# Eight resident GLA states instead of seven, with the stacked keys of both stream parities in one tile

## The chip, the core and the metric

The kernel runs on one core of a Trainium2 chip, in one launch. The metric is device time in microseconds. The core has a matrix engine (PE in the profile, with its weight loads as PEld), a vector engine (DVE), a scalar engine (ACT), a general engine (POOL), a queue engine (SP), and DMA engines that these feed. Each engine works through its own instructions in the order in which the program lists them and waits, by semaphores, for what the others produce. Three runs of the kernel before took 2575.13, 2565.62 and 2572.58 us; their median, 2572.58 us, is the time to compare with.

## What is computed

A step of a two-layer encoder. Layer 0 is stick-breaking attention, layer 1 gated linear attention (GLA). There is one new stream of 512 tokens (the prompt) and eight running streams of 16 new tokens each (the samples), all at width 2048. The change touches layer 1's samples. For each of 4 heads a stream has a state matrix of 256 x 512, which is read for the output, decayed, and extended by the new tokens' keys and values:

```python
def gla_chunk(S, inp):
    q, k, v, g = inp
    C = q.shape[1]
    b = jnp.cumsum(g, axis=1)
    b_last = b[:, -1]
    q_in = q * jnp.exp(b)
    a = jnp.einsum('bchd,bshd->bhcs', q_in, k * jnp.exp(-b))
    a = jnp.where(jnp.tril(jnp.ones((C, C), dtype=bool)), a, 0.0)
    o = jnp.einsum('bhcs,bshe->bche', a, v) + jnp.einsum('bchd,bhde->bche', q_in, S)
    S = jnp.exp(b_last)[..., None] * S + jnp.einsum('bshd,bshe->bhde', k * jnp.exp(b_last[:, None] - b), v)
    return S, o
```

The samples' states come in as `state_gla` and leave as the output `s_sample`, in float32. Each is cut into two pieces of 128 x 512 (256 KB), so 64 pieces pass through the core: 8 streams, 4 heads, 2 pieces. Two layer projections, normalisations and the output projection surround this.

## The kernel before

**The whole.** All products are made of float32 numbers split into a high and a low part (`halves`, L133 to L135), three matmuls for a product. The kernel has a main stream of matmuls (projections), and lanes of side work (attention, GLA) that it slips between them. In layer 1's GLA stage the main stream is first `plain` (L620 to L652; its matmuls are L641), which makes the remaining queries and keys with 320 columns a matmul, then `share` (L673 to L724; matmuls L687, 512 columns), which is the output projection head by head. The main stream's matmul output is `ps_mm`; the lanes use `ps_tp` and `ps_z`.

**Who sets the order.** PE's order is written by the kernel itself. `pe["now"]` is a running estimate of PE's time, and `Side.tick` (L316 to L333) lets a lane take its next step when the estimate has reached the time that the lane asked for with `step`. `Side.after` puts off a call by a given time. So what a lane asks for decides where in the main stream its matmuls stand. The orders of DVE, ACT, POOL and SP are made by a scheduler when the program is built. [...]

**The sample lane** (`sample_lane`, L1761 to L1846). For each head it makes queries (`qz`) and stacked keys, then goes through four groups n = 0 to 3. A group is one 128-row piece `dt` of the state (n // 2) and one parity `e` of the streams (n % 2), that is four states, of streams e, 2 + e, 4 + e and 6 + e. In a group:

- Four matmuls at L1825 read the four states for the output. Each has 32 columns of weights, and the four stand in four column strips of PE's array. In the profile they are 8 instructions, since a float32 matmul is two.
- Four matmuls at L1831 make the four updates, each of 512 columns. Their weights are `kst[e][:, m, :]` and the moving operand is `vst[:, m, :]`. `kst` is two tiles: in `kst0` only rows 0 to 47 hold keys, in `kst1` only rows 64 to 111; the other rows are zero. `vst` holds the values of even streams in rows 0 to 47 and of odd ones in rows 64 to 111. All 128 rows take part, and the zeros drop the other parity.
- DVE adds the update to the decayed state (L1833), and `leaves` (L1756) stores the state and, 7.0 units of the estimate later, asks for the next load.

**The states' places.** A state piece lies in a tile `s0` (called `s` in the profile) of a ring of `S0 = 7` tiles. Seven loads are asked for at the start (L1753), each later one by `leaves`. A load into a place must wait until the store of the state that was there has landed. Loads and stores of states, the gate tiles (`gate`, in and out), `vst` and the prompt's state `S` all go by `move` (L76 to L78), which is a DMA issued by POOL, so they stand in one line, in order, with POOL's small arithmetic (`on_r`, L234). A group waits in the estimate until all its four states have been asked for 8.0 units ago.

**The key tile.** `stack` (L1790 to L1807) transposes the keys into a bank and copies rows 0 to 47 with ACT and rows 64 to 111 with DVE into `kst[0]` and `kst[1]`.

**From `plain` to `share`.** When `plain` ends, `share` for head 0 needs four tiles of rows (`og_in`, loaded by SP, L1857), each split into `ogh` (ACT) and `ogl` (DVE). The prediction calls the stretch between the two the seam.

```python
                    for m in range(4):
                        yield step(0.3, tp=1)
                        pt = bank("tp")
                        l = kst[e][:, m, :]
                        mm(pt, l, by(l, vst[:, m, :]), start=True, stop=True)
```

## Time and profile before

| | |
|---|---|
| median of three runs | 2572.58 us |
| the profiled execution | 2576.88 us, of which the span from the first to the last instruction is 2575.1 us |
| PE busy | 2454.8 us (95%), 17369 matmuls |
| DVE, ACT, POOL busy | 1592.8, 1016.3, 163.4 us |
| GLA stage | from about 2050 us to 2452 us of the span |
| L1825 and L1831 in it | 128 and 64 instructions on PE |
| state loads and stores | 64 and 64, of 256 KB each, 4.5 and 4.0 us median from issue to landing |

A row of the timeline gives the start, the duration, the engine, the line, the operation, what is written and read, the shape and a count; in brackets how long the engine had been idle and what ended that. On PE a shape such as `128*32` is the rows and columns of weights. A matmul's end is modelled and overlaps the next one, so the time that a matmul takes from the engine is the distance between the starts of two rows, not the duration. In the rows on waits the columns are the engine, what it was about to write and its line, then what it waited for; total us, times, longest. In the rows by window: the window, its length, busy time (and instructions) of PE, PEld, DVE, ACT and POOL, the clock granted to PE as a share of full speed, the share of time that the DMA engines were busy, and GB/s.

### The profile page before, as it was taken

How to read it: one execution, taken by the hardware profiler on the slowest of the kernel's cores; microseconds unless marked ns; L12 is line 12 of the kernel's file. 1: busy time of each engine (PE TensorE's matmuls, PEld its weight loads, DVE VectorE, ACT ScalarE, POOL GpSimd, SP SyncE). 2: the span in 40 equal slices, each digit the busy share in tenths (PEclk: the TensorE clock that was granted, in tenths of full speed). 3: DMA queues.
4: the chain of work that ended last, by engine and by line, in shares of the span. 5: the costliest groups of instructions: out<-in, count | busy, mean ns of one | idle time of the engine just before them, and what ended most of it. 6: DMA issues, size and time to landing. Idle time of an engine off the chain costs nothing.

```text
span 2575.1 us, 43490 instructions
## 1 busy us (share of the span) xinstructions
PE 2454.8 (95%) x17369; PEld 2160.0 (84%) x17369; DVE 1592.8 (62%) x2469; ACT 1016.3 (39%) x1794; POOL 163.4 (6%) x385
## 2 busy tenths in 40 slices
PE   6899999999999999999999889999999999979998
PEld 4579999998999988777777767999999988857776
DVE  5565555555666656766776577665667565555456
ACT  4332222222223335565444344333333554555223
POOL 0010000000000000000000000000000233242000
PEclk7899999999999999999999999999999999989999
DMA  9956666766654366766665763345443777785633
GB/s 341 324 190 218 223 210 200 237 213 195 218 190 122 115 209 210 231 214 205 221 222 173 228 214 121 99 115 141 121 117 110 213 224 245 233 280 191 208 118 144
DMA packets 452797, 502.06 MB, mean 195 GB/s; under 512 B 26090, under 2 KB 349810, under 8 KB 452466
## 3 DMA queue, kind: packets, MB, share of 16 engines
q1 hardware_dynamic: 429634, 435.55, 53.5%
q0 software_dynamic: 16048, 51.92, 6.1%
q10 hardware_dynamic: 6912, 11.80, 1.2%
q8 instruction: 137, 2.24, 0.4%
q14 instruction: 66, 0.54, 0.1%
HBM read 410.05 MB, written 89.13 MB: 194 GB/s over the span
## 4 chain that ended last, share of the span: by engine, by line
PE 77%; DMA 9%; DVE 7%; issue 3%; ACT 3%; POOL 1%; SPq 0%; ACTq 0%; DVEq 0%; POOLq 0%
PE ps_mm L583 39%; PE ps_mm L687 10%; PE ps_mm L641 6%; PE ps_mm L367 3%; PE ps_mm L507 3%; DMA ar<-in_w_ada_dram 2%; PE ps_tp L1061 2%; PE ps_z L180 1%; PE ps_tp L1516 1%; PE ps_tp L1029 1%; PE ps_z L1005 1%; DVE wl L135 1%; DMA gv<-kr 1%; PE ps_tp L1106 1%; PE ps_mm L1965 1%
## 5 line engine op out<-in xcount | busy, mean ns | idle before, releaser
L583 PE MATMUL ps_mm<-sums,wh 128*128 128x320 f32 x2752 | 618.0, 313 | 5.8 <-ACT wh L134 5.8
L583 PEld LDWEIGHTS ps_mm<-sums,wh 128*128 128x128 f32 x2752 | 462.1, 189 | 14.9 <-ACT wh L134 7.1
L583 PE MATMUL ps_mm<-h,wh 128*128 128x320 f32 x2064 | 462.7, 312 | 3.0 <-DVE u L589 2.8
L583 PE MATMUL ps_mm<-sums,wl 128*128 128x320 f32 x1376 | 428.0, 311 | 1.0 <-DVE wl L135 1.0
L135 DVE TENSOR_TENSOR wl<-wr,wh 128x1024 fp32r<-128x1024 f32 x194 | 237.2, 1223 | 239.2 <-ACT wh L134 238.2
L583 PEld LDWEIGHTS ps_mm<-h,wh 128*128 128x128 f32 x2064 | 344.0, 188 | 19.0 <-issue 13.7
L134 ACT CAST wh<-wb 128x1024 fp32r<-128x1024 f32 x170 | 178.4, 1050 | 426.9 <-PE ps_mm L583 370.4
L134 ACT CAST wh<-wr 128x1024 fp32r<-128x1024 f32 x194 | 203.6, 1050 | 339.3 <-PE ps_mm L583 179.1
L583 PE MATMUL ps_mm<-h,wl 128*128 128x320 f32 x1032 | 319.4, 310 | 0.2 <-DVE wl L135 0.2
L641 PE MATMUL ps_mm<-h,wh 128*128 128x320 f32 x1152 | 268.7, 320 | 8.9 <-ACT wh L134 5.4
L583 PEld LDWEIGHTS ps_mm<-sums,wl 128*128 128x128 f32 x1376 | 260.5, 189 | 1.8 <-DVE wl L135 1.8
L135 DVE TENSOR_TENSOR wl<-wb,wh 128x1024 fp32r<-128x1024 f32 x170 | 207.7, 1222 | 60.9 <-ACT wh L134 60.5
L641 PEld LDWEIGHTS ps_mm<-h,wh 128*128 128x128 f32 x1152 | 195.7, 192 | 26.0 <-issue 12.1
L687 PE MATMUL ps_mm<-wh,ogh 128*128 128x512 f32 x460 | 200.0, 435 | 5.7 <-DVE y L692 2.8
L583 PEld LDWEIGHTS ps_mm<-h,wl 128*128 128x128 f32 x1032 | 194.2, 188 | 0.5 <-DVE wl L135 0.5
L687 PE MATMUL ps_mm<-wh,ogl 128*128 128x512 f32 x460 | 181.9, 395 | 0.5 <-DVE ogl L135 0.5
L687 PE MATMUL ps_mm<-wl,ogh 128*128 128x512 f32 x460 | 181.8, 395 | 0.0
L641 PE MATMUL ps_mm<-h,wl 128*128 128x320 f32 x576 | 180.1, 313 | 1.4 <-DVE wl L135 1.4
L687 PEld LDWEIGHTS ps_mm<-wh,ogh 128*128 128x128 f32 x460 | 87.6, 190 | 33.5 <-issue 16.5
L641 PEld LDWEIGHTS ps_mm<-h,wl 128*128 128x128 f32 x576 | 110.2, 191 | 2.1 <-DVE wl L135 2.1
L943 DVE TENSOR_TENSOR_SCAN k<-k,zero_c 128x544 f32<-128x544 f32 (+4 forms) x96 | 93.2, 975 | 29.4 <-ACT k L939 16.6
L687 PEld LDWEIGHTS ps_mm<-wh,ogl 128*128 128x128 f32 x460 | 87.1, 189 | 20.8 <-DVE ogl L135 0.9
(352 smaller groups left out, 3773.9 us busy)
## 6 DMA issues: line engine op xcount, KB each, us to landing
ar<-in_w_ada_dram SPq DMA_DIRECT2D x160, 512.0 KB
wb<-in_sb_w_in_dram SPq DMA_DIRECT2D x82, 512.0 KB
kc<-in_cache_sb_k_dram SPq DMA_DIRECT2D x64, 512.0 KB
vc<-in_cache_sb_v_dram SPq DMA_DIRECT2D x64, 512.0 KB
wr<-in_gla_w_in_dram SPq DMA_DIRECT2D x51, 512.0 KB
wb<-in_gla_w_in_dram SPq DMA_DIRECT2D x45, 512.0 KB
wr<-in_sb_w_in_dram SPq DMA_DIRECT2D x44, 512.0 KB
ar<-in_w_ada_dram SPq DMA_DIRECT2D x64, 256.0 KB
```

The lines of the kernel that those rows point to most:

```text
L134: nc.scalar.copy(hi, x)
L135: (e or dve).tensor_tensor(lo, x, hi.bitcast(F32), op=ALU.subtract)
L180: mm(acc[32 * q:32 * q + 32, :w], cT[:, kt + m, :], by(cT[:, kt + m, :], rs[m // each][:, m % each, q, :]), start=kt + m == 0, stop=kt + m ...
L367: mm(acc[a], l[:, c], by(l[:, c], r[:, k2, :]), start=kt == k0 and first, stop=kt == k0 + nk - 1 and last)
L507: mm(acc[a], l, by(l, r[:, e, :]), start=j == 0 and e == 0 and begun, stop=j == 7 and e == 1 and last)
L583: mm(acc, l[:, k, :], by(l[:, k, :], r), start=start and k == 0 and first, stop=k == 7 and last, skip_group_check=True)
L641: mm(acc[nt], l[:, k, :], by(l[:, k, :], r), start=k0 == 8 and k == 0 and first, stop=k0 == 0 and k == 7 and last)
L687: mm(acc, l, by(l, r[:, e, :]), start=i == 0 and e == 0 and first, stop=i == 1 and e == 1 and last)
L943: dve.tensor_tensor_scan(kr, kr, zeros[:, :w], 1.0, ALU.mult, ALU.add)
L1005: mm(z[:, :n], q[:, hh, qs], by(q[:, hh, qs], k[:, hh, :n]), start=True, stop=True)
L1029: mm(o[:, :P], l, by(l, aT[:, kb, :]), start=kb == 0, stop=kb == qb)
L1061: turn_block(tp[:, P * c:P * c + P], block(kc[:, c, P * hh:P * hh + P]), ident)
```

## The change

`S0` becomes 8. The place for the eighth state (512 float32 a partition) comes from `kst`, which is now one tile instead of two of that size: even streams' keys stay in its rows 0 to 47, odd ones' in 64 to 111, and each update's matmul takes only the 64 rows of its parity, of `kst` and of `vst`. One zeroing of a tile by POOL at the stage's start goes.

```diff
-S0 = 7
+S0 = 8
...
-        kst = [gl.tile([P, 4, P], F32R, name=f"kst{n}") for n in range(2)]
+        kst = gl.tile([P, 4, P], F32R, name="kst")
         vst = gl.tile([P, 4, 512], F32R, name="vst")
-        for t in qz + kst + [vst]:
+        for t in qz + [kst, vst]:
             nc.gpsimd.memset(t.bitcast(F32), 0.0)
...
-                        (dve.tensor_copy if e else nc.scalar.copy)(kst[e][r], tp[r].rearrange("p (m n) -> p m n", m=4))
+                        (dve.tensor_copy if e else nc.scalar.copy)(kst[r], tp[r].rearrange("p (m n) -> p m n", m=4))
...
-                        l = kst[e][:, m, :]
-                        mm(pt, l, by(l, vst[:, m, :]), start=True, stop=True)
+                        l = kst[64 * e:64 * e + 64, m, :]
+                        mm(pt, l, by(l, vst[64 * e:64 * e + 64, m, :]), start=True, stop=True)
```

The number of places is part of what the lane's requests depend on, so PE's order in the GLA stage moves too, and the orders of the other engines with it.

PE, head 0, from the last update of the first group on. The names are matmul output, moving operand and weights; a number tells one tile of a name from another, `s_...` being a state's place. Before:

```order
L1831 MATMUL ps_tp<-vst,kst_20571 128x512
L641 MATMUL ps_mm<-h,wh 128x320 x2
L641 MATMUL ps_mm<-h,wl 128x320
...
L1528 MATMUL ps_tp<-q,k 128x128 x2
L1676 MATMUL ps_tp<-ident,k 128x128 x2
...
L1825 MATMUL ps_z<-s_20593,qz_20570 32x512
L1825 MATMUL ps_z<-s_20595,qz_20570 32x512
L1825 MATMUL ps_z<-s_20597,qz_20570 32x512
L1825 MATMUL ps_z<-s_21319,qz_20570 32x512
```

And now:

```order
L1831 MATMUL ps_tp<-vst,kst 128x512
L1825 MATMUL ps_z<-s_20591,qz_20570 32x512
L1825 MATMUL ps_z<-s_20593,qz_20570 32x512
L1825 MATMUL ps_z<-s_20595,qz_20570 32x512
L1825 MATMUL ps_z<-s_20597,qz_20570 32x512
L641 MATMUL ps_mm<-h,wh 128x320 x2
L641 MATMUL ps_mm<-h,wl 128x320
...
L1563 MATMUL ps_tp<-ident,on 128x128 x4
L1831 MATMUL ps_tp<-vst,kst 128x512
```

The second group used to stand 24 main matmuls after the first one's last update, since its fourth state (`s_21319`) had to take a place that the first group left; it now follows at once. In every head groups 0 and 1 form a pair, and groups 2 and 3 form another, 84 main matmuls after the first one (45 of the longer ones in the last head).

PE at the seam, head 2, from the end of `plain` to the first matmuls of `share`. Before:

```order
L641 MATMUL ps_mm<-h,wl 128x320
L1831 MATMUL ps_tp<-vst,kst_20571 128x512 x4
L1563 MATMUL ps_tp<-ident,on 128x128 x4
L1600 MATMUL ps_tp<-alr_in,wa_22793 128x320 x2
L687 MATMUL ps_mm<-wh,ogh 128x512
L687 MATMUL ps_mm<-wl,ogh 128x512
L687 MATMUL ps_mm<-wh,ogl 128x512
L1825 MATMUL ps_z<-s_23397,qz_20570 32x512
L1825 MATMUL ps_z<-s_23399,qz_20570 32x512
L1825 MATMUL ps_z<-s_23401,qz_20570 32x512
L1825 MATMUL ps_z<-s_23496,qz_20570 32x512
```

And now:

```order
L641 MATMUL ps_mm<-h,wl 128x320
L1831 MATMUL ps_tp<-vst,kst 128x512
L1825 MATMUL ps_z<-s_23298,qz_20570 32x512
L1825 MATMUL ps_z<-s_23300,qz_20570 32x512
L1825 MATMUL ps_z<-s_23362,qz_20570 32x512
L1825 MATMUL ps_z<-s_23364,qz_20570 32x512
...
L1831 MATMUL ps_tp<-vst,kst 128x512 x2
L1600 MATMUL ps_tp<-alr_in,wa_22825 128x320 x2
L687 MATMUL ps_mm<-wh,ogh 128x512
L687 MATMUL ps_mm<-wl,ogh 128x512
L687 MATMUL ps_mm<-wh,ogl 128x512
```

Head 2's last group and its four updates stood inside `share`'s first products and now stand ahead of them.

POOL, the DMAs for that same group. A name ahead of the arrow is written, `out_7_dram` is the samples' state output, `out_6_dram` the prompt's; the group's states are 23397, 23399, 23401 and 23496 before, and 23298, 23300, 23362 and 23364 now. Before:

```order
L78 DMA s0_23401<-in_state_gla_dram 128x512
L234 TENSOR_TENSOR on_r_23365<-on_ms_23363,mhalf_79 128x1
L78 DMA og_2_93<-gate_23160 512x1x128
L78 DMA out_6_dram<-S_22871 128x2x512
L78 DMA out_7_dram<-s0_23222 128x512
L78 DMA gate_23425<-gr_3_106 128x4x128
L78 DMA out_7_dram<-s0_23287 128x512
L78 DMA out_7_dram<-s0_23289 128x512
L78 DMA out_7_dram<-s0_23373 128x512
L78 DMA og_2_93<-gate_23309 512x1x128
L78 DMA s0_23496<-in_state_gla_dram 128x512
```

And now:

```order
L78 DMA out_7_dram<-s0_22621 128x512
L78 DMA out_7_dram<-s0_22665 128x512
L78 DMA gate_23214<-gr_2_105 128x4x128
L78 DMA s0_23298<-in_state_gla_dram 128x512
L78 DMA s0_23300<-in_state_gla_dram 128x512
L78 DMA s0_23362<-in_state_gla_dram 128x512
L78 DMA s0_23364<-in_state_gla_dram 128x512
L234 TENSOR_TENSOR on_r_23290<-on_ms_23288,mhalf_79 128x1
```

The group's fourth load used to stand behind the four stores of the group just before it and two DMAs of `og`; now all four loads stand behind the stores of the pair before, and ahead of those of their own pair.

## The prediction

> **What bounds the kernel now.** I read the page first, then the stage that the change touches by windows, then the waits, then the timelines of PE, DVE and POOL around each wait. The page:
>
> ```profile
> PE 2454.8 (95%) x17369; PEld 2160.0 (84%) x17369; DVE 1592.8 (62%) x2469; ACT 1016.3 (39%) x1794; POOL 163.4 (6%) x385
> ```
>
> PE is the bound of the whole. The GLA stage by windows:
>
> ```profile
> 2050.00:2207.00 157.00, 153.75 (x982) 137.63 (x980) 94.37 (x170) 81.70 (x160) 51.11 (x86) 1.00 0.74 237
> 2207.00:2220.00 13.00, 8.58 (x37) 6.34 (x35) 6.03 (x14) 5.01 (x10) 4.45 (x9) 0.74 0.72 228
> 2220.00:2283.00 63.00, 63.00 (x400) 56.05 (x399) 36.62 (x67) 31.59 (x63) 20.99 (x36) 1.00 0.74 236
> 2283.00:2310.00 27.00, 11.83 (x34) 5.60 (x34) 16.95 (x28) 14.55 (x26) 10.35 (x17) 0.68 0.83 289
> 2310.00:2452.00 142.00, 138.13 (x638) 108.25 (x637) 76.39 (x121) 60.58 (x103) 30.94 (x53) 1.00 0.60 196
> ```
>
> Outside two holes, at 2207 and 2283, PE is full, and after both holes its clock is low for a while (0.74 and 0.68 as means). So time is won by closing holes, and any time that PE's own instructions gain in the full stretches is paid whole. Who makes the holes:
>
> ```profile
> POOL out_dram L78 <- DVE s L1833: 53.7, 20, 13.4
> POOL s L78 <- DMA out_dram<-s: 25.9, 18, 3.4
> PE ps_z L1825 <- DMA s<-in_state_gla_dram: 17.0, 2, 12.6
> ```
>
> PE waits 17.0 us in two pieces for a state's load, and POOL, which issues it, sits in its line for stores that wait for DVE, and for stores to land ahead of loads.
>
> **What the change takes away: the first hole.** PE there, and an undisturbed group of L1825 for comparison:
>
> ```profile
> 2073.82 0.40 PE L1516 MATMUL ps_z<-v,aNl 128*128 128x512 f32 x1
> 2074.15 1.07 PE L1825 MATMUL ps_z<-s,qz 128*32 128x512 f32 x8
> 2075.14 0.56 PE L641 MATMUL ps_mm<-h,wh 128*128 128x320 f32 x2
> 2075.54 0.31 PE L641 MATMUL ps_mm<-h,wl 128*128 128x320 f32 x1
> 2075.69 0.45 PE L641 MATMUL ps_mm<-h,wh 128*128 128x320 f32 x2
> 2075.98 0.31 PE L641 MATMUL ps_mm<-h,wl 128*128 128x320 f32 x1
> ```
>
> ```profile
> 2206.29 1.06 PE L1825 MATMUL ps_z<-s,qz 128*32 128x512 f32 x6
> 2211.77 1.92 PE L1825 MATMUL ps_z<-s,qz 128*32 128x512 f32 x2 [4.42 <-DMA s<-in_state_gla_dram]
> 2213.61 0.90 PE L641 MATMUL ps_mm<-h,wh 128*128 128x320 f32 x2
> 2216.60 0.31 PE L641 MATMUL ps_mm<-h,wl 128*128 128x320 f32 x1
> ```
>
> A group takes 2075.14 - 2074.15 = 0.99 us; this one took 2213.61 - 2206.29 = 7.32, so 6.33 are lost. Then PE runs at half speed until 2216.60: the same instructions, at the distances of undisturbed ones, would take about 1.7 instead of 2.99 us, which is 1.3 more. The hole costs 7.6 us. Its cause, with the group before on PE:
>
> ```profile
> 2194.19 1.07 PE L1825 MATMUL ps_z<-s,qz 128*32 128x512 f32 x8
> 2196.59 0.75 DVE L1833 SCALAR_TENSOR_TENSOR s<-s,es,ps_tp 128x512 f32<-128x512 f32 x1 [2.49 <-PE ps_tp L1831]
> 2203.44 1.12 POOL L78 DMA_DIRECT2D out_dram<-s  x2
> 2207.04 0.55 POOL L78 DMA_DIRECT2D s<-in_state_gla_dram  x1
> ```
>
> The state whose place is wanted was updated at 2197.3, stored from 2203.4, and reloaded from 2207.0 to 2211.8: 14.4 us from update to the next state, of which 6.1 were POOL's line, while the two groups' reads start 12.1 us apart. In the new order a place is wanted again two groups later. From the start of one pair to that of the next in the same head stand 170 instructions on PE, counted in the order; at the pace of the third window (63.00 us for 400) that is 27 us. In the last head it is 131, at the pace of the fifth window (142.00 for 638) 29 us. 27 against 14.4 leaves 12, so I take the wait as gone, and the low clock behind it with it. Three more groups lose a little, because their four matmuls did not start together:
>
> ```profile
> 2105.53 1.66 PE L1825 MATMUL ps_z<-s,qz 128*32 128x512 f32 x8
> 2119.61 1.45 PE L1825 MATMUL ps_z<-s,qz 128*32 128x512 f32 x8
> 2262.92 1.90 PE L1825 MATMUL ps_z<-s,qz 128*32 128x512 f32 x8
> ```
>
> Against 1.07 that is 0.59 + 0.38 + 0.83 = 1.8 us, which goes for the same reason.
>
> **The second hole, at the seam.** The wait there is the longer one, but something else is late just behind it:
>
> ```profile
> 2289.35 1.93 PE L1825 MATMUL ps_z<-s,qz 128*32 128x512 f32 x6
> 2303.87 1.92 PE L1825 MATMUL ps_z<-s,qz 128*32 128x512 f32 x2 [12.59 <-DMA s<-in_state_gla_dram]
> 2305.71 0.79 PE L687 MATMUL ps_mm<-wh,ogh 128*128 128x512 f32 x1
> 2309.97 0.39 PE L687 MATMUL ps_mm<-wh,ogh 128*128 128x512 f32 x1
> ```
>
> ```profile
> 2291.66 0.81 DVE L135 TENSOR_TENSOR ogl<-og_in,ogh 128x640 fp32r<-128x640 f32 x1
> 2298.29 0.82 DVE L135 TENSOR_TENSOR ogl<-og_in,ogh 128x640 fp32r<-128x640 f32 x1 [0.85 <-ACT ogh L134]
> 2302.84 0.83 DVE L135 TENSOR_TENSOR ogl<-og_in,ogh 128x640 fp32r<-128x640 f32 x1 [0.80 <-ACT ogh L134]
> ```
>
> `share`'s first accumulation needs the second, third and fourth `og` rows, ready at 2292.5, 2299.1 and 2303.7. Without the state's wait PE would do the second at 2292.5, the third at 2299.1, and the fourth from 2303.7, at the low clock (0.43 us a matmul), to 2305.0; with an update of 0.2 the next accumulation would begin at about 2305.2 instead of 2309.97. So of 12.6 us of wait only 4.8 are won; the rest of the hole stays, now as a wait for `og` rows. Bounds: nothing, if the rows come 5 us later than now; 15.4 (2305.71 less 2290.34, the undisturbed end of the group), if they come that much earlier. I take 4.8, since nothing in the rows' own chain (`og_in` loads by SP, then a split each) is edited.
>
> Together the change takes away 7.6 + 1.8 + 4.8 = 14.2 us.
>
> **What it adds: 64 updates in a half-height tile.** The moving operand keeps 512 columns, so L1831 itself is no shorter. What is new is that its weights fill 64 rows, between matmuls of 128. Two kinds of rows bound that. A matmul of 96 rows stands among others of 128 and costs only its columns (320 columns, 0.15 us to the next start, as for L641):
>
> ```profile
> 2313.67 0.31 PE L1600 MATMUL ps_tp<-alr_in,wa 96*128 96x320 f32 x1
> 2313.82 0.40 PE L687 MATMUL ps_mm<-wh,ogh 128*128 128x512 f32 x1
> ```
>
> And tiles of 32 columns cost something on the way in and out. In: 2074.15 - 2073.82 = 0.33 instead of the usual 0.23 for 512 columns, 0.10. Out: 0.40 to the second L641 row instead of 0.29, 0.11. Between: a run of twice the length shows the clean rate,
>
> ```profile
> 56.28 1.93 PE L180 MATMUL ps_z<-ar,cT 128*32 128x256 f32 x32
> 184.62 1.07 PE L222 MATMUL ps_z<-ar,cT 128*32 128x256 f32 x16
> ```
>
> 16 instructions of 256 columns, the work of L1825's 8 of 512, take 1.93 - 1.07 = 0.86, but the group took 0.99: 0.13. One visit to another tile shape costs 0.34 us. The weights now loaded on entry are 128 columns instead of 32:
>
> ```profile
> L1831 PEld LDWEIGHTS ps_tp<-vst,kst x64: 186/188/330, 2077.3 to 2391.4; 128*128 128x128 f32 x64
> L1825 PEld LDWEIGHTS ps_z<-s,qz x128: 106/109/155, 2074.1 to 2388.5; 128*32 128x32 f32 x128
> ```
>
> That may show 0.08 more, 0.42 in all. So a visit costs between 0 (the 96-row matmul) and 0.42; I take 0.38, the middle of 0.34 and 0.42, because a half-height tile is a tile of another shape like L1825's, and the 96-row one is likely still the full array. The Trainium skill speaks to this: TensorEngine Tiling (Array Packing), "Key Properties", says that a change of the tiling mode, not merely of the tile, drains the engine, and its list of modes has 64 x 128 apart from 128 x 128 and none of 96. By that rule the visit is paid, as in L1825's rows; the 96-row row does not contradict it; no row of this case shows a 64-row tile.
>
> How many visits: in the new order the 64 updates stand in 63 places, 55 of them followed by full-height matmuls and 8 by a group of L1825, which then is not entered from full height. That makes 63 + 55 + 8 - 8 = 118 more changes of shape, or 59 visits: 59 x 0.38 = 22.4 us. Three of the places are at the seam, where PE waits anyway (1.1 us hidden), so 21.3; bounds 0 and 59 x 0.42 = 24.8.
>
> **What costs nothing.** One zeroing by POOL (0.54 us) goes, ahead of loads that have 60 us of time. The eighth load comes at the start, 256 KB. The copies into `kst` write other rows than the ones being read and stand behind the same transposes. DVE, ACT and POOL do the same work.
>
> **Sum.** 21.3 - 14.2 = 7.1 us more. The profiled execution's 2576.88 would be 2584.0; it stands 4.3 above the median of the runs, and against 2572.58 the sum gives 2579.7 us. That is within 0.5% (12.9 us), about what a measurement of this kernel can tell from no change; the three runs shown lie 9.5 apart.
>
> **Rivals.**
>
> *The half-height tile is free.* For it speaks the 96-row matmul; against it the 32-column rows. Then the 14.2 us are all gain: 2558.4, faster by 0.55%. Chance 0.2, of which I count 0.13 as faster by over 0.5%.
>
> *Slower: the seam gives nothing.* In the new order head 2's last four updates and their DVE additions stand just ahead of the splits of the `og` rows, and two loads of `v` stand ahead of the third row in SP's line. If the fourth row is ready 5 us later (the spread of these loads is as large: the rows became ready 6.6 and 4.6 us apart), the 4.8 are lost, and with the upper price of a visit the sum is 24.8 - 1.2 - 9.4 = 14.2 more, and with rows later still up to 19: 2587 to 2592. It decides from the point where price less gain passes 12.9. Against it: POOL's line has less to wait for, and ACT's at the seam hang on it. Chance 0.22.
>
> *The holes stay, elsewhere.* The pairs want eight states close together, and POOL's line still holds stores, gates and `vst` in order; another of POOL's waits like the 13.4 us one above would use up the 12 us. If half of the 9.4 us gained outside the seam came back as other waits for states, the sum would be 11.8 more, 2584.4, and a hole of 3 us or more would bring a low clock again: 2587. Against it: the 27 and 29 us. Chance 0.08, of which 0.02 stay within 0.5%.
>
> **How the numbers follow.** The forecast has 0.5, with its own range 2572 to 2587 (seam from 0 to 10, visits 0.34 to 0.42). The range reaches down to the free tile, 2558, less 2 for a somewhat better seam, and up to 2590, within the slower rival: 2556 to 2590. Same: the forecast without its edges, 0.45, the part of the free tile below 0.5%, 0.07, and 0.02 of the third rival: 0.54. Faster: 0.13 of the free tile and 0.02 of the forecast, for a seam much better than thought: 0.15. Slower: 0.22 and 0.06 of the rivals and 0.03 of the forecast, for its upper edge: 0.31.
>
> **What would show each step.** The visits: in the new profile the distance from L1831 to the next matmul, now 0.23, and the entry to it; right if together they are some 0.4 us over the old. The first hole: no wait of L1825 for a state's load over 1 us. The seam: PE's longest wait there named `ogh` or `ogl`, about 11 us in all. The forecast is wrong if L1831 stays at 0.23 on both sides, or if waits for states of several us remain.

## The result, and the profile after

| | before | after |
|---|---|---|
| median of the runs (on the same chip) | 2572.68 us of 4 | 2592.92 us of 4 (2589.78 to 2594.05) |
| ratio, with its 95% interval | | 1.0079 (1.0061 to 1.0097) |
| the profiled execution, its span | 2576.88, 2575.1 us | 2593.62, 2591.9 us |
| first L1825 to first matmul of the last part (L367) | 2074.15 to 2451.78: 377.6 us | 2069.32 to 2470.18: 400.9 us |

The change makes the kernel 20.2 us slower, 0.79%. The prediction was 2579.7 us, with a range that ends at 2590. The stage between the two matmuls of the last line has grown by 23.2 us, more than the two executions differ in all (16.8): after reaches the stage 4.8 us sooner and is 1.6 us shorter behind it. Those two parts are not explained here. Over the fourteen kernels the profiled executions reach the stage between 2064.5 and 2075.1 us.

The page of after, its line of totals:

```profile
PE 2471.2 (95%) x17369; PEld 2155.8 (83%) x17369; DVE 1596.2 (62%) x2469; ACT 1016.2 (39%) x1794; POOL 163.6 (6%) x384
```

PE is busy 16.4 us longer with the same 17369 matmuls: some of them take longer, by their own cost or by a lower clock. The stage of after by windows, cut at its own holes (columns as before: window, length, busy time of PE, PEld, DVE, ACT, POOL, PE's clock, DMA share, GB/s):

```profile
2050.00:2124.00 74.00, 73.98 (x435) 59.57 (x433) 44.83 (x81) 39.95 (x77) 24.22 (x42) 1.00 0.70 218
2124.00:2136.00 12.00, 5.18 (x24) 5.19 (x25) 6.52 (x14) 3.84 (x10) 3.93 (x7) 0.72 0.76 259
2136.00:2290.00 154.00, 152.59 (x917) 127.25 (x916) 84.83 (x147) 72.01 (x137) 51.16 (x85) 1.00 0.73 235
2290.00:2325.00 35.00, 19.88 (x70) 12.84 (x70) 18.92 (x32) 16.34 (x29) 15.69 (x27) 0.71 0.88 292
2325.00:2470.00 145.00, 139.85 (x611) 103.83 (x609) 74.08 (x116) 59.16 (x101) 23.44 (x39) 0.99 0.49 167
```

The hole at 2207 is gone. There is one now at 2124, where before had only a short wait, and the seam's hole (2290 to 2325) is as wide as it was. Who makes the holes, in the waits of after over the stage:

```profile
POOL out_dram L78 <- DVE s L1833: 79.7, 31, 12.6
...
PE ps_tp L1563 <- ACT on L1545: 21.4, 4, 8.4
```

No wait of PE for a state's load is left (17.0 us before). In its place PE waits 21.4 us, in four pieces, at L1563: the transposes of `on`, the normalised output of a head, which ACT scales at L1545 with the factor `on_r` that POOL computes at L234. And POOL waits 79.7 us for updates that it is to store, where it was 53.7. (A wait is named after what ended it; what that one had been waiting for is looked up below.)

A visit to the half-height tile, in the timeline of PE after:

```profile
2286.49 0.40 PE L1516 MATMUL ps_tp<-S1h,qcl 128*128 128x512 f32 x1
2286.82 0.49 PE L1831 MATMUL ps_tp<-vst,kst 64*128 64x512 f32 x1
2287.24 0.56 PE L641 MATMUL ps_mm<-h,wh 128*128 128x320 f32 x2
2287.64 0.31 PE L641 MATMUL ps_mm<-h,wl 128*128 128x320 f32 x1
```

0.33 us from L1516 to L1831 where 0.23 is usual, 0.42 from there to L641 (0.23), 0.40 over two L641 (0.29): 0.10 + 0.19 + 0.11 = 0.40 more. Over the single visits that wait for nothing the median is 0.39.

The new hole, in the timeline of all engines of after; the last update of head 0 is at 2115.51:

```profile
2117.54 0.15 DVE L232 TENSOR_SCALAR on_ms<-oss 128x1 f32<-128x1 f32 x1
...
2117.93 0.75 POOL L78 DMA_DIRECT2D og<-gate  x1 [4.49 <-DVE on_ms L232]
...
2121.70 0.51 POOL L78 DMA_DIRECT2D vst<-gv  x1 [0.44 <-issue]
...
2123.68 0.31 PE L641 MATMUL ps_mm<-h,wl 128*128 128x320 f32 x1
...
2124.80 0.58 POOL L78 DMA_DIRECT2D out_dram<-s  x1 [1.26 <-DVE gate L1564]
...
2125.99 0.78 POOL L234 TENSOR_TENSOR on_r<-on_ms,mhalf 128x1 f32<-128x1 f32 x1
...
2129.15 0.74 ACT L1624 ACTIVATE y<-b 128x640 f32<-128x640 f32 x1 [0.89 <-DVE q L1626]
...
2130.08 0.68 ACT L1545 ACTIVATE on<-ps_z,on_r 128x512 f32<-128x512 f32 x1
...
2130.82 1.12 PE L1563 MATMUL ps_tp<-ident,on 128*128 128x128 f32 x4 [6.83 <-ACT on L1545]
...
2131.58 0.88 PE L641 MATMUL ps_mm<-h,wh 128*128 128x320 f32 x2
```

Read it from the end. `on` is scaled at 2130.08, behind the exponentials of the next head's decays (L1624) in ACT's line. Its factor could have been made at 2117.69, but stood in POOL's line behind loads, stores and the next head's values, until 2125.99. DVE's line has a part ahead of that: ACT had the sum of squares ready at 2112.62, and `on_ms`, which is made from it, ran 4.9 us later. The same steps in before, in its timeline of all engines:

```profile
2123.71 0.13 DVE L232 TENSOR_SCALAR on_ms<-oss 128x1 f32<-128x1 f32 x1
...
2125.32 0.39 PE L1831 MATMUL ps_tp<-vst,kst 128*128 128x512 f32 x1
...
2128.43 0.62 POOL L234 TENSOR_TENSOR on_r<-on_ms,mhalf 128x1 f32<-128x1 f32 x1
...
2129.09 0.69 ACT L1545 ACTIVATE on<-ps_z,on_r 128x512 f32<-128x512 f32 x1 [2.42 <-POOL on_r L234]
...
2135.95 0.60 PE L1563 MATMUL ps_tp<-ident,on 128*128 128x128 f32 x4
```

There `on_ms` ran 1.7 us behind the sum, and ACT had been idle for 2.42 us when the factor came. In both kernels 48 main matmuls stand on PE between the head's last update and L1563. They covered the way in before (update 2125.32, `on` ready 2129.78, L1563 at 2135.95), and don't in after (2115.51, 2130.76, 2130.82).

The seam of after, in the timeline of all engines:

```profile
2295.18 0.57 POOL L234 TENSOR_TENSOR on_r<-on_ms,mhalf 128x1 f32<-128x1 f32 x1
...
2298.17 0.39 PE L687 MATMUL ps_mm<-wh,ogl 128*128 128x512 f32 x1
...
2305.59 0.72 ACT L134 CAST ogh<-og_in 128x640 fp32r<-128x640 f32 x1 [5.02 <-DMA og_in<-og]
...
2306.22 0.68 ACT L1545 ACTIVATE on<-ps_tp,on_r 128x512 f32<-128x512 f32 x1
...
2306.95 1.11 PE L1563 MATMUL ps_tp<-ident,on 128*128 128x128 f32 x4 [8.39 <-ACT on L1545]
...
2309.73 0.80 PE L687 MATMUL ps_mm<-wh,ogh 128*128 128x512 f32 x1 [0.38 <-ACT ogh L134]
...
2316.46 0.68 ACT L1545 ACTIVATE on<-ps_z,on_r 128x512 f32<-128x512 f32 x1
...
2317.20 1.11 PE L1563 MATMUL ps_tp<-ident,on 128*128 128x128 f32 x4 [5.82 <-ACT on L1545]
...
2322.72 0.39 PE L687 MATMUL ps_mm<-wh,ogl 128*128 128x512 f32 x1
```

The 12.6 us for a state have become 8.4 and 5.8 us for two pieces of `on`, a prompt's and the sample's, which now stand among `share`'s first products, and the full rate comes back only at 2322.7.

The two pieces have different causes. For the first, POOL had the factor ready at 2295.75; L1545 then stood in ACT's line behind the split of the third `og` row, for whose load ACT waited 5.02 us until 2305.59. So the 8.4 us that are named `on` end with an `og` row, and PE's next products needed that row too. For the second, the factor was ready at 2309.87, and L1545 came at 2316.46, behind the next head's decays and two more splits in ACT's line.

So the theory that the experiments had to test was: the visits cost what was forecast, the state waits go as forecast, and a new kind of wait, for `on`, gives all of that gain back. (At the seam 8.4 us of that wait are an `og` row's, as just read.) The rival: the half-height tile, or the eighth place itself, costs more than it seems.

### The profile page after: what moved, and what is told of

It is laid out like the page before. It is cut to its first block, busy times and chain, and to the rows that moved or that the text cites. A ratio compares the mean times of both kernels' runs of the same rounds, so it can differ in the third digit from the quotient of the medians.

```text
span 2591.9 us, 43502 instructions
## 1 busy us (share of the span) xinstructions
PE 2471.2 (95%) x17369; PEld 2155.8 (83%) x17369; DVE 1596.2 (62%) x2469; ACT 1016.2 (39%) x1794; POOL 163.6 (6%) x384
## 4 chain that ended last, share of the span: by engine, by line
PE 76%; DMA 8%; DVE 7%; issue 3%; ACT 3%; POOL 1%; SPq 1%; ACTq 0%; POOLq 0%; DVEq 0%
PE ps_mm L583 38%; PE ps_mm L687 10%; PE ps_mm L641 6%; PE ps_mm L367 3%; PE ps_mm L507 3%; DMA ar<-in_w_ada_dram 2%; PE ps_tp L1061 2%; DMA gv<-kr 1%; PE ps_z L180 1%; PE ps_tp L1029 1%; PE ps_tp L1516 1%; PE ps_z L1005 1%; DVE wl L135 1%; PE ps_tp L1106 1%; PE ps_mm L1965 1%
## 5 line engine op out<-in xcount | busy, mean ns | idle before, releaser
L641 PE MATMUL ps_mm<-h,wh 128*128 128x320 f32 x1152 | 274.2, 325 | 10.1 <-ACT wh L134 5.3
L641 PEld LDWEIGHTS ps_mm<-h,wh 128*128 128x128 f32 x1152 | 193.9, 193 | 32.4 <-issue 20.3
L641 PE MATMUL ps_mm<-h,wl 128*128 128x320 f32 x576 | 181.2, 314 | 1.4 <-DVE wl L135 1.4
L641 PEld LDWEIGHTS ps_mm<-h,wl 128*128 128x128 f32 x576 | 111.0, 193 | 2.1 <-DVE wl L135 2.1
L687 PEld LDWEIGHTS ps_mm<-wh,ogl 128*128 128x128 f32 x460 | 87.9, 191 | 21.3 <-DVE ogl L135 1.2
```

The lines of the kernel that those rows point to most:

```text
L641: mm(acc[nt], l[:, k, :], by(l[:, k, :], r), start=k0 == 8 and k == 0 and first, stop=k0 == 0 and k == 7 and last)
L687: mm(acc, l, by(l, r[:, e, :]), start=i == 0 and e == 0 and first, stop=i == 1 and e == 1 and last)
```

## The experiments

Each kernel was timed beside the kernel before on the same chip. A difference in us is the ratio less 1, times 2572.6; between two of the kernels it is the difference of their ratios, and by the two intervals it is good to about 4 to 6 us.

| | places | updates on | groups | ratio to before (95%) | us |
|---|---|---|---|---|---|
| after | 8 | 64 rows | in pairs | 1.0079 (1.0061 to 1.0097) | +20.3 |
| e1 | 7 | 64 rows | as before | 1.0066 (1.0052 to 1.0079) | +17.0 |
| e4 | 8 | 128 rows | in pairs | 1.0014 (1.0001 to 1.0026) | +3.6 |
| e10 | 8 | 128 rows | apart | 0.9951 (0.9936 to 0.9967) | -12.6 |
| e13 | 8 | 64 rows | apart | 1.0022 (1.0008 to 1.0036) | +5.7 |

The other kernels are variants around these. The orders of DVE, ACT, POOL and SP are made anew for each kernel and differ in places even where PE's order is the same.

**e1, the half-height tile alone.** After with the old number of places; PE's instructions stand in the order of before.

```diff
-S0 = 8
+S0 = 7
```

> Seven places, one key tile, updates on 64 rows: PE's order is word for word that of before, only the 64 updates are in a half-height tile. Theory (the visits cost, the order is a wash): 59 visits at 0.39 us are 23.0, of which some 1.6 at the seam lie in waits, so about 21 us over the kernel before, near 2594. Rival (the half-height tile is cheap in itself, and the new order of after makes most of the loss): within 8 us of before, 2573 to 2581.

2587.84 us, 17.0 more than before. Since PE's order is the same, the same instruction can be looked up in both traces: where PE waits for nothing, each group of four updates makes it 1.56 us later, 0.39 a visit. The difference shrinks again where before has a hole: at the first one the state no longer comes late for the slower PE, and the waits for states are two of 14.6 us in all, almost all at the seam:

```profile
PE ps_z L1825 <- DMA s<-in_state_gla_dram: 14.6, 2, 14.2
```

The rival falls, and 17.0 (13.4 to 20.3) is somewhat less than the 21 expected. The visits are most of the loss, and they cost less than 23.0 in all because some of them lie in a time in which PE would have waited: across the first hole PE's lag behind before falls from 6.0 to 0.6 us, and its wait of 2.4 us for `k` (L1626) is gone. The wait at the seam has not shrunk; it is 14.2 us, where it was 12.6.

**e4, the eighth place alone.** Two key tiles and full height as before; the room comes from the second place of `wa`, whose next load is asked for only after the last use of the one before it. PE's instructions stand in the order of after.

```diff
-S0 = 7
+S0 = 8
...
-                wa2 = gl.tile([96, 256], F32R, tag="wa2", name="wa2", bufs=2)
+                wa2 = gl.tile([96, 256], F32R, tag="wa2", name="wa2")
```

> Eight places, but two key tiles and updates on all 128 rows as before; the room comes from the second place of wa (1 KB) and what was free. PE's order is word for word that of after, without one half-height matmul. Theory (the state waits that go, 9.4 us, are given back as new waits for on and for og, some 9 us): within 4 us of before, 2569 to 2577. The prediction's own sum: 14.2 us faster, 2558.5. If instead the order of eight places is worse by itself, over 2580.

2574.52 us, 3.6 more than before (0.3 to 6.7): the prediction's gain of 14.2 is not there, though no wait for a state is left. PE's waits in e4:

```profile
PE ps_tp L1563 <- ACT on L1545: 15.8, 3, 8.2
PE ps_mm L687 <- ACT ogh L134: 7.0, 2, 6.3
```

At the seam (8.2 us) the sample's L1545 stands behind two splits of rows on ACT, which had waited 2.0 and 1.3 us for their loads, so that part of this wait too is the rows'.

With e1 it splits the result: 17.0 for the visits and 3.6 for the order make 20.6, and after is 20.3.

**e3, half the visits.** After, with the updates two at a time.

```diff
                     for m in range(4):
-                        yield step(0.3, tp=1)
+                        if m % 2 == 0:
+                            yield step(0.6, tp=2)
```

> After, with the four updates of a group issued two at a time instead of one by one, so 28 visits to the half-height tile instead of 59, for the same 64 updates. Theory (the price is paid per change of tile shape): 31 x 0.39 = 12 us less than after, about 2581, give or take 4 for a PE order that moves a little. Rival (the price is paid per update in the half-height tile): as after, 2593.

2599.23 us, ratio 1.0116 (1.0102 to 1.0129): slower than after, so the time missed both expectations. The visit with two updates has a median of 0.86 us, of which two times 0.23 are the updates: 0.40 a visit, the same as for one, so the price is one of the change of shape and not of the update. But PE's order moved too: head 0's last update comes 38.2 us behind the stage's first L1825, where it is 46.2 in after, and PE's waits in the stage are 45.7 us in all, where they are 28.7. Most of the growth is in the waits named `on`:

```profile
PE ps_tp L1563 <- ACT on L1545: 32.5, 4, 17.5
```

**e5, 96 rows.** After, with the even streams' updates on rows 0 to 95.

```diff
-                        l = kst[64 * e:64 * e + 64, m, :]
-                        mm(pt, l, by(l, vst[64 * e:64 * e + 64, m, :]), start=True, stop=True)
+                        r = slice(64, 128) if e else slice(0, 96)
+                        l = kst[r, m, :]
+                        mm(pt, l, by(l, vst[r, m, :]), start=True, stop=True)
```

> After, with the even streams' updates on rows 0 to 95 instead of 0 to 63 (rows 64 to 79 then add products of odd streams' keys to even streams' states: a part of the computation is changed); odd streams' updates stay on 64 rows. Theory (a tile of another shape is what costs, not empty rows): even updates cost PE 0.23 us from the start before to the start after beyond their neighbours' own, as in the kernel before, odd ones 0.62; about 28 x 0.39 = 11 us less than after, near 2582. Rival (any matmul that leaves rows of the array empty costs a drain): both kinds 0.62, and the time of after.

2584.10 us (ratio 1.0053, 1.004 to 1.0067). By the ratios that is 6.7 us less than after, where 11 were expected; the wide uncertainty of that difference allows 11. Both kinds of update stand in one profile, in the groups by form (busy us and mean ns of one):

```profile
L1832 PE MATMUL ps_tp<-vst,kst 64*128 64x512 f32 x32 | 15.6, 492 | 0.0
L1832 PE MATMUL ps_tp<-vst,kst 96*128 96x512 f32 x32 | 13.0, 405 | 0.0
```

From the start before to the second start behind, less what the neighbours usually take, an update on 96 rows takes 0.24 us as in before, and one on 64 rows 0.62 to 0.63. Empty rows are free; another tile shape costs 0.39.

**e6, the transposes later.** On the kernel of e4, a sample's L1563 is asked for later.

```diff
-                yield step(7.0, tp=1)
+                yield step(14.0, tp=1)
                 leave(h, NP, on, g)
                 through["s"] = h + 1
                 if h + 1 < GH:
-                    yield step(4.0)
+                    yield step(0.3)
```

> Eight places, two key tiles and updates on 128 rows (the kernel of e4), with the sample lane's transposes of on asked for 14.0 units after on is asked for instead of 7.0, and the next head's fetch 0.3 behind them instead of 4.0. Theory (the new order's loss is PE standing at L1563 for a sample's on): the waits at the end of heads 0 and 1 go, 6.4 and 1.3 us, with some 1.5 of low clock; the one at the seam, 8.2, only passes to the fourth og row. So 8 to 9 us less than e4, 2565 to 2567. Rival (a closed hole just opens as another one, of the next late thing): as e4, 2574 to 2575.

2567.89 us, ratio 0.999 (0.998 to 1.0): 6.2 less than e4 (about 2 to 10), where 8 to 9 were expected. At the end of head 0 `on` is ready as late behind its `on_ms` as in e4 (2111.71 to 2124.62, 12.9 us, as 2113.66 to 2126.57), but L1563 comes at 2126.65 and waits for nothing. The samples' waits at heads 0 and 1 are gone; a prompt's `on` now makes PE wait 10.8 us at the seam. For the hole at the end of head 0 it is the place of L1563 against `on` that counts. But the rival has a part too, since a new hole of 9.1 us opens soon behind, in the timeline of all engines of e6:

```profile
2146.90 0.69 ACT L1545 ACTIVATE on<-ps_tp,on_r 128x512 f32<-128x512 f32 x1 [9.96 <-POOL on_r L234]
...
2148.05 0.30 ACT L1798 CAST kc<-kd 128x128 fp32r<-128x128 f32 x1
...
2148.73 0.69 PE L1804 MATMUL ps_tp<-ident,kc 128*128 128x128 f32 x2 [9.06 <-DVE kc L1799]
```

PE waits for `kc`, the next head's keys on their way to `kst`; their first step on ACT stands behind a prompt's L1545, and that had waited 9.96 us for POOL's factor. It is the same pair of lines under another name.

**e7, POOL's line shorter.** On the kernel of e4, `vst` is filled by DMAs from SP.

```diff
-                        move(vst[r0:r0 + NT].bitcast(F32), rows)
+                        load(vst[r0:r0 + NT].bitcast(F32), rows)
```

> The kernel of e4 with the six DMAs that fill vst for a head issued by SP instead of POOL; PE's order is the same word for word. Theory (on comes late because POOL's small arithmetic on_r stands in POOL's line behind DMAs): with 3 us of issues and 1 to 3 us of their waits gone from ahead of on_r, it runs some 4 us sooner behind on_ms at the end of head 0, and PE's wait there falls from 6.4 to about 3; 3 to 5 us less than e4, near 2570. Rival (ACT's line ahead of L1545 decides, not POOL's): wait and time as in e4, 2574.5. If SP's weights are held up by the waits of vst, slower than e4.

2572.18 us, ratio 1.0 (0.9987 to 1.0013): 3.6 less than e4, the size expected, but not clear of the noise of that difference, and not in the way expected. The chain at the end of head 0 in e7, in the timeline of all engines:

```profile
2109.58 0.15 DVE L232 TENSOR_SCALAR on_ms<-oss 128x1 f32<-128x1 f32 x1
...
2118.44 0.57 POOL L234 TENSOR_TENSOR on_r<-on_ms,mhalf 128x1 f32<-128x1 f32 x1
...
2119.04 0.69 ACT L1545 ACTIVATE on<-ps_z,on_r 128x512 f32<-128x512 f32 x1 [3.54 <-POOL on_r L234]
...
2119.78 1.12 PE L1563 MATMUL ps_tp<-ident,on 128*128 128x128 f32 x4 [3.40 <-ACT on L1545]
```

`on_r` comes 8.9 us behind `on_ms`, no sooner than in e4 (8.1): state loads and stores hold POOL's line just as long. What is better is ACT, whose order happens to have L1545 ahead of the decays' exponentials, so that it runs at once. PE's wait there is 3.4 us, where it was 6.4, but the one at the end of head 1 is 4.3, where it was 1.3. Both lines take part at the end of head 0: from `on_ms` to the factor it takes 8 to 9 us in POOL's, and from the factor to L1545 3.3 us in ACT's in e4 and after.

**e8, both edits,** of e6 and e7, on the kernel of e4.

> Both edits, of e6 and of e7, on the kernel of e4. Theory: the waits for on at heads 0 and 1 are gone by the first edit, so the second adds only what POOL's shorter line gives the og rows at the seam, 0 to 3 us: 2562 to 2567. Rival: 2574.

2569.82 us, ratio 0.9992 (0.9979 to 1.0004). No better than e6: the two edits don't add up, and in the stage PE now waits for `on` at three lines (10.8 us, of which 6.1 for a prompt's at L1563), for `ogh` (3.8) and for DVE's `k` (2.9) instead.

**e9, later transposes in before.** The edit of e6 on the kernel before.

> The kernel before (seven places) with the transposes of a sample's on asked for later as in e6. Theory: before has no wait of PE for on over 1.5 us, so the edit wins nothing there: within 3 us of before, 2568 to 2574, and the state waits (17.0 us on L1825) stay. Rival (later transposes are worth the same in any order): 8 us less than before, 2563.

2574.87 us, ratio 1.0013 (1.0 to 1.0027), 3.3 more than before. Later transposes are worth nothing where no one waits for `on`. The state waits did not stay as expected, though: 7.3 us in place of 17.0, with 5.9 us for `ogh` at the seam and 3.5 for `kc` instead.

Up to here every full-height kernel lay between 2568 and 2575. What was common to e4 to e8 was the pairs. The section on the kernel says that a group waits until its states have been asked for 8.0 units ago. As `tick` is written (L316 to L333), that wait does not hold here: the lane's step for the last update is taken in the first loop, the lane's new request is then in the list `due` that was made ahead of it, and as a request for a tiled step it is run in the same tick, whatever time it asked for. So with seven places it was the eighth state, not yet asked for, that held the second group back; with eight, nothing does.

**e10, the groups apart.** The kernel of e4, with groups at least 12.0 units apart, about what they have in before.

```diff
-                    while any(x not in states for x in group):
+                    while any(x not in states for x in group) or pe["now"] < since:
                         yield step(0.3)
                     yield step(max(since, max(states[x][1] for x in group) + 8.0) - pe["now"], tiled=True)
+                    since = pe["now"] + 12.0
```

> The kernel of e4 (eight places, updates on 128 rows), with the sample lane's groups held at least 12.0 units of the estimate apart, so that they no longer come in pairs; PE's order is then close to that of before, but each load has an eighth place to go to. Theory (the pairs, not the eighth place, make the new waits: a head's samples end 10 us earlier, on top of the next head's decays, and eight stores at once fill POOL's line): PE's waits for on shrink to under 3 us in all, no state wait over 1 us, 9 to 14 us less than before, 2556 to 2561. Rival (the waits have a common floor that no order of the groups changes, set by the og rows and the decays): within 5 of before, 2565 to 2575.

2560.42 us, 12.6 less than before (8.5 to 16.5 by the interval), and faster than before and after. PE's two longest waits in the stage of e10:

```profile
PE ps_mm L687 <- ACT ogh L134: 10.3, 2, 9.1
PE ps_mm L367 <- DVE y L692: 2.0, 1, 2.0
```

And the longer piece of the first, in the timeline of all engines:

```profile
2282.25 1.87 PE L1826 MATMUL ps_z<-s,qz 128*32 128x512 f32 x8
...
2291.21 0.69 ACT L1545 ACTIVATE on<-ps_z,on_r 128x512 f32<-128x512 f32 x1 [3.14 <-POOL on_r L234]
2291.80 0.73 ACT L1624 ACTIVATE y<-b 128x640 f32<-128x640 f32 x1
...
2292.42 1.34 ACT L134 CAST ogh<-og_in 128x640 fp32r<-128x640 f32 x2
...
2293.19 0.80 PE L687 MATMUL ps_mm<-wh,ogh 128*128 128x512 f32 x1 [9.07 <-ACT ogh L134]
```

No wait for a state, and of PE's own for `on` only 0.2 us; the seam's wait is named `ogh` and is 10.3 us. Its longer piece is no late row, though. ACT takes up the two splits without a wait for their loads, right behind a decay's exponential and a sample's L1545, which had waited 3.14 us for POOL's factor: ACT's and POOL's lines are in it again. The group of states that waited 12.6 us at this place in before (now L1826) runs without a break. From its first such group (2075.07) to L367 (2438.23) the stage takes 363.2 us, 14.5 less than in before. At the end of head 0 the old spacing is back: the last update comes 50.7 us behind the first group (51.2 in before, 41.0 in e4), from `on_ms` to L1545 it takes 4.5 us (2123.18 to 2127.68; 5.4 in before, 12.2 in e4), and L1563 at 2134.39 waits for nothing. The rival, a floor that no order changes, falls.

**e11, e10 with the edit of e7.**

> The kernel of e10 with the DMAs that fill vst issued by SP as in e7. Theory: POOL's line is no longer what PE waits for once the groups are apart, so nothing more than 3 us off e10 in either direction. Rival (POOL's line is the common cause in every order): 4 to 9 us less than e10, as e7 was against e4.

2567.29 us, ratio 0.997 (0.9956 to 0.9983): slower than e10 by 5 us if anything, with 11.7 us of waits for `ogh` where e10 has 10.3, and a stage of 370.1 us. That is not clear of the noise, so the first expectation is not excluded; the rival falls. The six DMAs of `vst` are not the part of POOL's line that limits e10. The line itself still counts: at the seam of e11 ACT again waits 2.95 us for POOL's factor ahead of the two splits, and PE waits 8.9 us for `ogh`.

**e12, a third place for the `og` rows.** On e10. The diff shows the edits for the third place alone.

```diff
-                    t.append(gl.tile([P, T], F32, tag="pl", name="pl", bufs=2))
+                    t.append(gl.tile([P, T], F32, tag="pl", name="pl", bufs=3))
...
-                rows[kt] = gl.tile([P, T], F32, tag="pl", name="og_in", bufs=2)
+                rows[kt] = gl.tile([P, T], F32, tag="pl", name="og_in", bufs=3)
...
-                    if kt % 4 < 3 and kt < 9 and came["plain"]:
-                        ask_rows(kt + 1)
+                    for n in (1, 2):
+                        if kt % 4 + n < 4 and kt + n < 10 and came["plain"]:
+                            ask_rows(kt + n)
```

> The kernel of e10 with a third place for the og rows (tile pl) and two rows asked for ahead instead of one. The room for it comes from one key tile that is read on all 128 rows, so each state takes in the update of the other parity's stream too (a part of the computation is changed), and from one mask tile. Theory (what is left of the seam is the og rows, one after another through two places): the rows are ready 5 to 8 us earlier and the seam shrinks by 4 to 8 us against e10. Rival (the loads of the rows share the DMA engines with everything else and come no sooner for a third place): as e10.

2561.74 us, ratio 0.9959 (0.9943 to 0.9975), which is e10's time. The wait for `ogh` is gone from PE's list: ACT splits the third and fourth rows at 2276.24 and 2280.15, ahead of the sample's L1545. But ACT's `y` (4.1 us) and DVE's `k` (2.8 us) make PE wait near there instead; the stage is 362.1 us. The longer wait for `y` (3.2 us) ends with a copy on ACT at 2288.91 that stood behind the same L1545, which had waited 7.46 us for POOL's factor. So the time is the rival's, by another reason than the rival's, and what is left of the seam is not the rows alone. (e12 also has one mask tile less; whether that takes part was not tried.)

**e13, after with its groups apart.** The edit of e10 on after itself.

> After itself (eight places, one key tile, updates on 64 rows), with nothing changed but the groups held 12.0 units apart as in e10; PE's order is that of e10 word for word. Theory (visits and pairs add up, and the pairs alone made the loss that the prediction missed): e10's 12.6 us below before, plus 60 visits at 0.39 us, 23.4, less 2 to 4 us that lie in waits: 7 to 9 us over before, about 2580, and 12 to 13 less than after. Rival (the slower PE of the half-height tile hides the waits of the pairs anyway): within 4 us of after, 2589 to 2593.

2578.46 us, 5.7 more than before (2.1 to 9.3), where 7 to 9 were expected, and 14.6 less than after. PE's longest waits are again those of e10:

```profile
PE ps_mm L687 <- ACT ogh L134: 8.1, 3, 6.2
PE ps_mm L367 <- DVE y L692: 2.0, 1, 2.0
```

So the half-height tile costs 17.0 us with seven places (e1), 16.7 in pairs (after against e4) and 18.3 apart (e13 against e10); the pairs cost 16.2 at full height (e4 against e10) and 14.6 at half height (after against e13); the eighth place without pairs wins 12.6. The sum of the three, 18.3 + 14.6 - 12.6, is after's 20.3 by construction; that the same edit gives nearly the same from either side is what the runs add. By single executions the stage agrees: 377.6 us in before, 391.5 in e1 (2070.47 to 2461.97), 383.9 in e4 (2071.01 to 2454.94), 400.9 in after, 363.2 in e10 and 383.6 in e13 (2072.75 to 2456.30).

## Why the prediction was wrong, point by point

- **The price of a visit** was right: 0.38 taken, 0.39 measured. 96 rows of 128 cost nothing, 64 rows cost 0.39. The Trainium skill, TensorEngine Tiling (Array Packing), "Key Properties", says that a change of the tiling mode drains the engine. The traces agree with that; the price is theirs. The way in and the way out are those taken from the 32-column tiles; the middle is 0.19 where 0.13 was read, and that this comes from the wider weights, as the prediction had it, was not tried. The rival of a free tile is out.
- **How much of it is paid** was put at 21.3, with 1.1 hidden at the seam. By the runs it is 17 to 18 of 23.0: 5 to 6 us of visits lie in times at which PE would have waited. With seven places that is at the first hole and not at the seam (e1); with the groups apart the seam's wait does shrink, to 8.1 us in e13 from 10.3 in e10.
- **The first hole** was right: after has no wait of PE for a state, the longest in any kernel with eight places is 1.02 us (e3), and from 2136 to 2290 PE has its full clock in after.
- **The seam** failed in after. The prediction gave it 4.8 us, with the rest of its hole as a wait for `og` rows, about 11 us. That wait is there, as 8.4 us under the name of `on`, which stood behind the third row's split, and 0.4 under its own. What was not forecast is the 5.8 us for the sample's `on` and the low clock until 2322.7, and nothing is won. In e10 the longest wait has the name and, with 10.3 us, about the size that were forecast, but that is luck: its longer piece ends with ACT's line behind `on`, and not with the load of a row.
- **The step that failed** is the one in "What costs nothing": "DVE, ACT and POOL do the same work." They do, but at another time. The new order ends a head's samples earlier (head 0's last update comes 51.2 us behind the stage's first L1825 in before, 41.0 in e4, 46.2 in after), with eight updates and stores close together, while the next head's decays fill ACT. From `on_ms` to `on` it takes 12.5 us at the end of head 0 where it took 5.4, and the 48 main matmuls in front of L1563 no longer cover it. The pairs were seen in the order and were costed at nothing for every wait but that of the states. They cost 14.6 to 16.2 us. By the traces after loses 17.3 us in the stage against e13: 9.5 of them up to the last L641, where `on` holds PE for 7.2 us with a low clock behind it, 3.9 from there to `share`'s 45th matmul, and 3.8 behind that.
- **The rivals.** "The holes stay, elsewhere" had the right place, POOL's line and the pairs, and the right kind of loss, a hole that passes to another wait. But it looked only at states, allowed half of the 9.4 us, and had a chance of 0.08. The slower rival at the seam came near the right size, but its mechanism, later `og` rows, did not happen: its loads of `v` do stand ahead of the third row's in SP's line, yet against `share`'s first matmul the third and fourth rows were split no later (8.6 and 11.9 us behind it in after, 9.5 and 14.0 in before).
- **The sum.** Gains of 14.2 and costs of 21.3 made 7.1. With the groups apart, so that the pairs do nothing, the same change gives -14.5 in the trace and -12.6 in the runs at full height, and +5.7 at half height (e13, 2578.46 us). The two mechanisms were there at about their forecast sizes, the seam's part of the gain by luck; a third one of about 15 us was missing.

That the pairs make the loss is shown by e10 and e13, and the way from them to PE is read in the traces. How their 16 us divide between the lines of POOL, ACT and DVE is open: e7 changed the first two at once, since the engines' orders are made anew for each kernel, and no run took DVE's apart. That no other effect of the pairs takes part, such as the share of time that the DMA engines are busy (0.88 at the seam of after), was not tried.

## What to carry to other kernels

More buffers do not only take a wait away; they also let whoever was held back by it run ahead, and work that used to be spread arrives at once. So ask of a released stage where its results go next, what stands in line there, and how much work on the bound engine covers that way; if the old spacing was good, write it down as a rule of its own instead of leaving it to the shortage (e10 is the eighth place, with its room taken from `wa`, and one such line). A wait carries the name of what ended it: before you act on the name, look at what stood ahead of that instruction in its own engine's line. Here a wait for `on` was an `og` row's load, and a wait for `ogh` was in part `on`. And before cutting an operand to fewer rows to save room, look whether the tile shape changes: 96 of 128 rows were free, 64 cost 0.39 us each time.

## What the runs showed of the hardware

- A single matmul on a 64 x 128 tile among full ones costs 0.39 us more than on 96 or 128 rows: 0.10 on the way in, 0.19 to the next matmul and 0.11 over the one after. Two such matmuls in a row cost 0.40 together. The ways in and out are those of the 32-column tile that the prediction used (0.10 in, 0.11 out), though the weights are four times as wide.
- A slower PE can lose less than its own sum: in e1 PE is 6.0 us later than in before ahead of the first hole and 0.6 us later behind it.
